# SSM rotation sums on GpSimd, a float32 output operator, q scaled early, reloads into finished heads' slots, and tables in three tiles

## Chip, core and metric

The kernel runs on one core of a Trainium2 chip. The metric is the device time of one execution in microseconds. Five engines work side by side, each through its own instructions in order: TensorE (PE, matmuls; PEld is its weight load), VectorE (DVE), ScalarE (ACT), GpSimd (POOL) and SyncE (SP, which mostly issues DMAs). 'ACTq', 'SPq' and so on are an engine's issuing side.

## What is computed

One layer of a hybrid encoder over 512 positions of width 1024:

```python
h = h + 0.5 * swiglu(rms_norm(h, ffn1_norm), ffn1_w_gate, ffn1_w_up, ffn1_w_down)
u = rms_norm(h, mix_norm)
q, k, v, x_ssm, g_attn, g_ssm = split(u @ w_in)        # 8 q heads, 2 kv heads of 64
q, k = rope(rms_norm(q)), rope(rms_norm(k))
y_attn = softmax(q @ k.T * 64 ** -0.5) @ v @ w_attn_branch
y_s5 = s5(x_ssm, forward) + s5(x_ssm, backward) + ssm_d * x_ssm
z = gelu(y_s5)
z = z * sigmoid(z @ ssm_glu_w + ssm_glu_b)
y_ssm = z @ w_ssm_branch
h = h + (sigmoid(g_attn) * y_attn + sigmoid(g_ssm) * y_ssm) @ w_out
h = h + 0.5 * swiglu(rms_norm(h, ffn2_norm), ...)
h = h + sigmoid(rms_norm(h, ple_norm) @ ple_w_gate) * (p @ ple_w_proj)
```

`s5` is a linear recurrence with complex diagonal states: 32 groups of 16 channels, 64 states each, in both directions.

## The kernel before

Activations are held transposed, features on the 128 partitions and the 512 positions in the free dimension. A float32 matmul is done as three products of halves: `split` (ACT L554, DVE L555) makes a high and a low part, and `mm3` (L569 to L571) multiplies high by high, low by high and high by low. A weight chunk `w` comes in by a DMA on SP (L564) and is split the same way. For the SSM, `split3` (L32 to L38) cuts a float32 tile into three bf16 tiles, two casts on ScalarE and two subtractions on VectorE, and `mm6` (L41 to L45) makes one product of them with six bf16 matmuls.

The span falls into FFN1 (0 to 408 us), the mixing stage (408 to 765), FFN2 (777 to 1122) and the input embedding at the end. FFN1 runs the generator `ssm_params` beside it: after each part of its own work it lets the generator go on by a credit (`side`). The generator makes, from the layer's parameters, four operators of the SSM and writes them to DRAM: `wv` (input), `wo` (output), `m` (within a chunk) and the tables `tb` of rotations and decays. For the tables, eight tiles `tst` of 128x1280 are filled, the last fifth `dv` by VectorE (L303 to L305), the rest by ScalarE (L307 to L309), and written out by ScalarE's queue (L310). The tiles share the tag `w3` with two buffers. On GpSimd's queue go the DMAs that reorder the operators' factors (L240 to L251).

In the mixing stage the SSM runs in 16 blocks of two groups (`ssm_block`). SP loads a block's `wv`, `tbl`, `wo` and `m` (L441 to L449). TensorE forms `pv` with 24 bf16 matmuls. VectorE rotates: `tt` is one 128x512 product (L471), and a difference and a sum of 128x128 make `vv` of it (L472, L473). Two scans over 64 partitions each, forward and backward, make the states W (L481, L482). `te` (L485) and another sum and difference (L486, L487) rotate back and give E. `split3` cuts E in three, and TensorE adds into `py` twelve matmuls of `m` and 24 of `wo`. ScalarE makes GELU of it (Z, L978).

Among the blocks stand other projections: q's norm and rope, the transposes `qt` and `kt`, and the gates, 16 in all. A gate is 24 matmuls of 512 columns (`pi`), a product on VectorE (L835) and a tanh on ScalarE. Behind the blocks the eight heads follow, scores (L957, L958), maximum (L959), its scale (L960), exp (L962, with its scale `rq`), four transposes at a time (`ppt`, L1002) and values (`po`, L1007, L1008); the remaining gates and the SSM branch (`pg`) are run among them as `fill`. Z goes through DRAM to be transposed: SP writes it in eight DMAs (L985), and `z_load` fetches it in four pieces `zT` on GpSimd's queue (L1034) into slots of the normed input `xg`, which the gates read until their end. ScalarE and VectorE split each piece into `z`.

The order of the instructions on each engine is set by a scheduler of the tile framework when the kernel is built; `high_priority` puts the SSM blocks ahead. A tile with `bufs` 1 can be written again only when its last reader is done.

Of the kernel before, what the change touches and what calls it, by code (L numbers as in the profile page):

```python
# [45 lines left out]
def ssm_params(tc, nc, pk_, px, dp, k):  # L46
# [6 lines left out]
    d["wo"] = dp.tile([NB, P, 3 * GB * 2 * P], BF16, name="d_wo")  # L53
# [221 lines left out]
    for gh in range(0, G, GH):  # L275
        T = pw.tile([P, 2, GH, NC_ + 2], F32, tag="T", name=f"T{gh}")
        V.memset(T[:, :, :, 0], 0.0)
        V.memset(T[:, :, :, NC_ + 1], 0.0)
# [4 lines left out]
        n = 1
        tb = pw.tile([P, 2, 2, GH * NC_ // 2], F32, tag="tb", name=f"tbx{gh}")
        while n < NC_:
            br = rkl[:, 0].unsqueeze(2).broadcast_to([P, GH, n])
# [4 lines left out]
            if n < NC_:
                sq = pw.tile([P, 2, GH], F32, tag="sq", bufs=2, name=f"sq{gh}_{n}")
                ta = pw.tile([P, 2, 2, GH], F32, tag="sqt", name=f"sqt{gh}_{n}")
                cmul2(sq[:, 0], sq[:, 1], rkl, rkl[:, 0], rkl[:, 1], ta)
# [42 lines left out]
    for b in range(NB):  # L337
        gs = slice(b * GB, (b + 1) * GB)
        x4 = lambda t: t[:, gs].unsqueeze(3).broadcast_to(sh)
        y4 = lambda t: t[:, gs].unsqueeze(2).broadcast_to(sh)  # L340
# [72 lines left out]
    for b in range(NB):  # L413
# [22 lines left out]
def ssm_prefetch(nc, sp, k, j):  # L436
# [16 lines left out]
def ssm_block(nc, sp, px, pre, U, j):  # L453
# [64 lines left out]
def kernel(  # L518
# [427 lines left out]
    def scores(hd):  # L946
# [273 lines left out]
```

## Time and profile before

| what | value |
|---|---|
| median of three runs | 1187.05 us (1185.81 to 1188.17) |
| the profiled execution's own time | 1185.39 us |
| its span in the profile | 1183.6 us |
| TensorE, matmuls | 1143.2 us busy, 97% of the span |
| TensorE, weight loads (beside matmuls) | 943.5 us, 80% |
| VectorE | 774.0 us, 65% |
| ScalarE | 507.5 us, 43% |
| GpSimd | 58.5 us, 5% |
| mean granted clock of TensorE | 0.987 of full speed |

The busy shares are means over stages that differ much; the windows in the rows below show the stages. A window's row gives each engine's busy time with its number of instructions in brackets, then TensorE's granted clock as a share of full speed, the mean busy share of the DMA engines and what they moved.

### The profile page before, as it was taken

How to read it: one execution, taken by the hardware profiler on the slowest of the kernel's cores; microseconds unless marked ns; L12 is line 12 of the kernel's file. 1: busy time of each engine (PE TensorE's matmuls, PEld its weight loads, DVE VectorE, ACT ScalarE, POOL GpSimd, SP SyncE). 2: the span in 40 equal slices, each digit the busy share in tenths (PEclk: the TensorE clock that was granted, in tenths of full speed). 3: DMA queues.
4: the chain of work that ended last, by engine and by line, in shares of the span. 5: the costliest groups of instructions: out<-in, count | busy, mean ns of one | idle time of the engine just before them, and what ended most of it. 6: DMA issues, size and time to landing. Idle time of an engine off the chain costs nothing.

```text
span 1183.6 us, 16482 instructions
## 1 busy us (share of the span) xinstructions
PE 1143.2 (97%) x6150; PEld 943.5 (80%) x6150; DVE 774.0 (65%) x1574; ACT 507.5 (43%) x919; POOL 58.5 (5%) x95
## 2 busy tenths in 40 slices
PE   8999989999999999978898999999999999999998
PEld 7888868888788888867676788888888888888886
DVE  4986798887589848989666867554443344444542
ACT  6484455444345437443656634342322223223331
POOL 1314100000000000000010000000000000000100
PEclk9999999999999999999997999999999999999999
DMA  8739865545968995887552245333323433323422
GB/s 190 171 92 313 256 221 178 161 142 107 271 228 268 298 193 157 250 251 224 132 86 62 45 105 164 88 98 91 89 74 99 128 100 96 88 64 98 157 57 54
DMA packets 253440, 175.97 MB, mean 149 GB/s; under 512 B 34896, under 2 KB 235792, under 8 KB 253360
## 3 DMA queue, kind: packets, MB, share of 16 engines
q1 hardware_dynamic: 246352, 153.20, 46.1%
q0 software_dynamic: 5392, 15.36, 5.0%
q10 hardware_dynamic: 1616, 6.36, 1.6%
q8 instruction: 48, 0.79, 0.3%
q14 instruction: 32, 0.26, 0.1%
HBM read 148.89 MB, written 37.58 MB: 158 GB/s over the span
## 4 chain that ended last, share of the span: by engine, by line
PE 74%; DVE 9%; DMA 8%; SPq 3%; issue 3%; ACT 2%; POOL 0%; ACTq 0%; DVEq 0%; POOLq 0%
PE pg L569 7%; PE pg L571 7%; PE pg L570 7%; PE pd L569 7%; PE pd L571 7%; PE pd L570 7%; PE pu L571 5%; PE pu L569 5%; PE pu L570 5%; DMA d_tb<-tst 2%; SPq L411 1%; PE pge L571 1%; PE po L569 1%; PE po L570 1%; PE po L571 1%
## 5 line engine op out<-in xcount | busy, mean ns | idle before, releaser
L723 DVE TENSOR_TENSOR t<-pu,rb 128x512 f32<-128x512 f32 x44 | 30.4, 692 | 86.4 <-PE pu L571 86.3
L721 DVE TENSOR_TENSOR t<-pg,rb 128x512 f32<-128x512 f32 x44 | 30.4, 691 | 54.6 <-PE pg L571 52.3
L554 ACT CAST ah<-t 128x512 fp32r<-128x512 f32 x44 | 27.3, 621 | 36.6 <-DVE t L724 35.9
L742 DVE SCALAR_TENSOR_TENSOR h<-pd,h 128x512 f32<-128x512 f32 x32 | 22.1, 690 | 30.5 <-PE pd L571 30.5
L722 ACT ACTIVATE t<-t 128x512 f32<-128x512 f32 x44 | 27.8, 632 | 28.4 <-DVE t L721 27.3
L555 DVE TENSOR_TENSOR al<-t,ah 128x512 fp32r<-128x512 f32 x44 | 30.3, 689 | 6.7 <-ACT ah L554 6.6
L724 DVE TENSOR_TENSOR t<-t,t 128x512 f32<-128x512 f32 x44 | 30.4, 691 | 2.3
L959 DVE TENSOR_REDUCE nb<-sc 128x1 f32<-128x512 f32 x32 | 21.7, 686 | 9.0 <-PE sc L958 8.9
L555 DVE TENSOR_TENSOR pl<-ppt,ph 128x512 fp32r<-128x512 f32 x32 | 22.0, 687 | 7.6 <-ACT ph L554 7.6
L554 ACT CAST ph<-ppt 128x512 fp32r<-128x512 f32 x32 | 18.8, 588 | 18.5 <-PE ppt L1002 18.4
L962 ACT ACTIVATE p<-sc,nb,rq 128x512 f32<-128x512 f32 x32 | 24.9, 781 | 3.8 <-DVE nb L960 3.5
L1125 POOL DMA_DIRECT2D pin<-in_p_dram x8 | 4.1, 524 | 400.4 <-PE pd L570 395.3
L579 ACT ACTIVATE xh<-h,gains 128x512 fp32r<-128x512 f32 x24 | 17.4, 724 | 14.0 <-DVE h L742 13.5
L1007 PE MATMUL po<-ph,vhl 128*128 128x512 f32 x32 | 14.3, 446 | 7.6 <-ACT ph L554 7.6
L43 PE MATMUL py<-E,wol 128*128 128x64 bf16 x384 | 18.6, 199 | 2.6 <-DVE E L36 2.2
L1002 PE MATMUL ppt<-ident,p 128*128 128x128 f32 x128 | 20.8, 277 | 0.0
L1002 PEld LDWEIGHTS ppt<-ident,p 128*128 128x128 f32 x128 | 16.6, 143 | 4.6 <-issue 0.2
L43 PEld LDWEIGHTS <-wol 128*128 128x128 bf16 x384 | 15.0, 101 | 5.3 <-issue 3.8
L43 PE MATMUL pv<-U,wv 128*128 128x64 bf16 x384 | 13.9, 193 | 5.4 <-DMA wv<-d_wv 5.4
L43 PEld LDWEIGHTS <-wv 128*128 128x128 bf16 x384 | 12.1, 98 | 7.8 <-DMA wv<-d_wv 6.0
L580 DVE SCALAR_TENSOR_TENSOR xl<-h,gains,xh 128x512 fp32r<-128x512 f32 x24 | 18.0, 749 | 0.4
L33 ACT CAST E<-vv 128x256 bf16<-128x256 f32 x16 | 6.5, 404 | 25.6 <-DVE vv L487 25.4
(1974 smaller groups left out, 3909.7 us busy)
## 6 DMA issues: line engine op xcount, KB each, us to landing
w<-in_ffn_w_gate_dram SPq DMA_DIRECT2D x44, 512.0 KB
w<-in_ffn_w_up_dram SPq DMA_DIRECT2D x44, 512.0 KB
w<-in_w_in_dram SPq DMA_DIRECT2D x26, 512.0 KB
w<-in_ffn_w_down_dram SPq DMA_DIRECT2D x32, 384.0 KB
w<-in_ffn_w_down_dram SPq DMA_DIRECT2D x32, 320.0 KB
d_wo<-wo SPq DMA_DIRECT2D x8, 768.0 KB
d_wv<-wv SPq DMA_DIRECT2D x8, 768.0 KB
wv<-d_wv SPq DMA_DIRECT2D x16, 384.0 KB
```

The lines of the kernel that those rows point to most:

```text
L43: nc.tensor.matmul(o, a[i], b[j], start=start and n == 0, stop=stop and n == 5)
L554: S.copy(hi, src)
L555: V.tensor_sub(lo, src, hi.bitcast(F32))
L569: T.matmul(o, ah, bh, start=start, stop=False)
L570: T.matmul(o, ah, bl, start=False, stop=False)
L571: return T.matmul(o, al, bh, start=False, stop=stop)
L721: V.tensor_mul(t1, gu[0], rb)
L722: S.activation(t1, t1, AF.Silu)
L723: V.tensor_mul(t2, gu[1], rb)
L724: V.tensor_mul(t1, t1, t2)
L962: S.activation(p_, sc, AF.Exp, bias=nb[:, t:t + 1], scale=rq[:, t, hd:hd + 1], accum_out=sm[:, t:t + 1])
L1002: T.transpose(pt[:, t * P:(t + 1) * P], pr[t][:, kt * P:(kt + 1) * P], ident)
```

## The change

Six edits. The sums of `vv` and E go from VectorE to GpSimd. The `wo` operator is written to DRAM in float32 (512 KB for four groups in place of 768), E is no longer split, and one float32 matmul takes the place of six bf16 ones, four a block. `wv` gets a second buffer in the blocks; in FFN1 the tile `wt` gets a second one, and `bd` and `bd3` go from two to one. The tables are filled in three tiles, `dv`, `st0` and `st1`, each with two buffers and a DMA of its own, `dv`'s on GpSimd's queue. q is multiplied by `rq` right after rope, so that the maximum's product (L960) and the scale of exp go. `zT` is loaded on SP's queue into the slots of q's heads 0 to 3, once each head is done, and `hb` is loaded early.

```diff
-    d["wo"] = dp.tile([NB, P, 3 * GB * 2 * P], BF16, name="d_wo")
+    d["wo"] = dp.tile([NB, P, GB * 2 * P], F32, name="d_wo")
...
         for b in range(gh // GB, (gh + GH) // GB):
-            st = pw.tile([P, TW], F32, tag="w3", bufs=2, name=f"tst{b}")
...
-            dv = v(4)
+            dtb = d["tb"][b].rearrange("p (i n) -> p i n", i=5)
+            dv = pw.tile([P, GB, NC_], F32, tag="dv", bufs=2, name=f"dv{b}")
             V.tensor_copy(dv, e8[:, b * GB:(b + 1) * GB].unsqueeze(2).broadcast_to([P, GB, NC_]))
...
-            for ri in range(2):
-                nc.scalar.copy(v(ri), T[:, ri, g0:g0 + GB, 1:NC_ + 1])
-                nc.scalar.copy(v(2 + ri)[:NS], T[:NS, ri, g0:g0 + GB, 0:NC_])
-                nc.scalar.copy(v(2 + ri)[NS:], T[NS:, ri, g0:g0 + GB, 2:NC_ + 2])
-            nc.scalar.dma_start(d["tb"][b], st)
+            nc.gpsimd.dma_start(dtb[:, 4], dv.rearrange("p g c -> p (g c)"))
+            gs = slice(b * GB - gh, (b + 1) * GB - gh)
+            for i in range(2):
+                st = pw.tile([P, 2, GB, NC_], F32, tag=f"st{i}", bufs=2, name=f"tst{b}_{i}")
+                for ri in range(2):
+                    if i == 0:
+                        nc.scalar.copy(st[:, ri], T[:, ri, gs, 1:NC_ + 1])
+                    else:
+                        nc.scalar.copy(st[:NS, ri], T[:NS, ri, gs, 0:NC_])
+                        nc.scalar.copy(st[NS:, ri], T[NS:, ri, gs, 2:NC_ + 2])
+                nc.scalar.dma_start(dtb[:, 2 * i:2 * i + 2], st.rearrange("p r g c -> p r (g c)"))
...
-    bds = [pw.tile([P, 2, GB, 2, CH], F32, name=f"bd{i}") for i in range(2)]
+    bds = [pw.tile([P, 2, GB, 2, CH], F32, name=f"bd{i}") for i in range(1)]
...
-        wt = pw.tile([P, GB, 2, L, CH], F32, tag="wt", name=f"wo{b}")
+        wt = pw.tile([P, GB, 2, L, CH], F32, tag="wt", bufs=2, name=f"wo{b}")
...
+        nc.sync.dma_start(d["wo"][b], wt.rearrange("p g r l c -> p (g r l c)"))
...
-        nc.sync.dma_start(d["wo"][b], w3.rearrange("p i g r m -> p (i g r m)"))
...
-    wv = sp.tile([P, 3, GM, 2 * P], BF16, tag="wv", name=f"wv{j}")
+    wv = sp.tile([P, 3, GM, 2 * P], BF16, tag="wv", bufs=2, name=f"wv{j}")
...
-    wo = sp.tile([P, 3, GM, 2 * P], BF16, tag="wo", bufs=2, name=f"wol{j}")
+    wo = sp.tile([P, GM, 2 * P], F32, tag="wo", bufs=2, name=f"wol{j}")
...
     V.tensor_mul(tt, b2(pv2), bb(0))
-    V.tensor_sub(vv[:, 0], tt[:, 0, 0], tt[:, 1, 1])
-    V.tensor_add(vv[:, 1], tt[:, 0, 1], tt[:, 1, 0])
+    nc.gpsimd.tensor_sub(vv[:, 0], tt[:, 0, 0], tt[:, 1, 1])
+    nc.gpsimd.tensor_add(vv[:, 1], tt[:, 0, 1], tt[:, 1, 0])
...
-    V.tensor_add(E[:, 0], tt[:, 0, 0], tt[:, 1, 1])
-    V.tensor_sub(E[:, 1], tt[:, 0, 1], tt[:, 1, 0])
-    E3 = [sp.tile([P, 2, N], BF16, tag=f"E{i}", bufs=2, name=f"E3{j}_{i}") for i in range(3)]
-    split3(nc, sp, E, E3, "vv", f"Er{j}", 3)
+    nc.gpsimd.tensor_add(E[:, 0], tt[:, 0, 0], tt[:, 1, 1])
+    nc.gpsimd.tensor_sub(E[:, 1], tt[:, 0, 1], tt[:, 1, 0])
...
-            mm6(nc, o, [wo[:, i, g, ri * P:(ri + 1) * P] for i in range(3)],
-                [e[:, ri, g * NC_:(g + 1) * NC_] for e in E3], False, ri == 1)
+            nc.tensor.matmul(o, wo[:, g, ri * P:(ri + 1) * P], E[:, ri, g * NC_:(g + 1) * NC_],
+                             start=False, stop=ri == 1)
...
+        for t in range(TT):
+            V.tensor_mul(qs[t], qs[t], rq[:, t].unsqueeze(2).broadcast_to([P, NH, HD]))
...
-            V.tensor_mul(nb[:, t:t + 1], nb[:, t:t + 1], rq[:, t, hd:hd + 1])
             p_ = slot(pool_p[hd % 2], "pp", 4, "p")
-            S.activation(p_, sc, AF.Exp, bias=nb[:, t:t + 1], scale=rq[:, t, hd:hd + 1], accum_out=sm[:, t:t + 1])
+            S.activation(p_, sc, AF.Exp, bias=nb[:, t:t + 1], accum_out=sm[:, t:t + 1])
...
+    def z_fetch(m):
+
+        zTs.append(slot(mp, f"q{m}", 1, "zT"))
+        nc.sync.dma_start(zTs[m], zs_d[m * P:(m + 1) * P])
...
-            zT = xs_(4 + m, "l", "zT")
-            nc.gpsimd.dma_start(zT, zs_d[m * P:(m + 1) * P])
...
     for hd in range(NH):
+        for m in {1: (0,), 2: (1, 2), 3: (3,)}.get(hd, ()):
+            z_fetch(m)
         run(values(hd), fill(hd), *([scores(hd + 1)] if hd < NH - 1 else []))
```

The scheduler moves much more than the diff. On VectorE, among the SSM blocks, a pair of blocks before reads:

```order
L485 TENSOR_TENSOR te_6090<-W_6085,tbl_6047 128x512 [waits DVE_49]
L471 TENSOR_TENSOR tt_6175<-pv_6150,tbl_6142 128x512 [waits DMAHW3_49]
L477 MEMSET W_6275 64x1 [waits DVE_49]
L478 MEMSET W_6275 64x1
L486 TENSOR_TENSOR vv_6091<-te_6090 128x128
L487 TENSOR_TENSOR vv_6091<-te_6090 128x128
L34 TENSOR_TENSOR Er_6098<-vv_6091,E_0_6095 128x256 [waits Activation_49]
L472 TENSOR_TENSOR vv_6176<-tt_6175 128x128
L473 TENSOR_TENSOR vv_6176<-tt_6175 128x128
L481 SCALAR_TENSOR_TENSOR W_6180<-tbl_6142,vv_6176 64x256 [waits DMAHW4_49,DVE_49]
L482 SCALAR_TENSOR_TENSOR W_6180<-tbl_6142,vv_6176 64x256
L36 TENSOR_TENSOR E_2_6097<-Er_6098,E_1_6096 128x256 [waits Activation_49]
```

and in the change:

```order
L489 TENSOR_TENSOR te_5807<-W_5802,tbl_5764 128x512 [waits DVE_49]
L475 TENSOR_TENSOR tt_5864<-pv_5839,tbl_5831 128x512 [waits DMAHW1_49,PE_49]
L481 MEMSET W_5936 64x1 [waits DVE_49]
L482 MEMSET W_5936 64x1
L485 SCALAR_TENSOR_TENSOR W_5869<-tbl_5831,vv_5865 64x256 [waits DMAHW2_49,Pool_49]
L486 SCALAR_TENSOR_TENSOR W_5869<-tbl_5831,vv_5865 64x256
```

`tt` is the first rotation's product, `te` the second's, W the scans, and `Er` and `E_2` the split of E. The four sums and two split steps have left VectorE's order; `te` and the next block's `tt` follow one another, and the scan behind them waits for GpSimd (`Pool_49`). On GpSimd, where no work of the blocks stood, now stands for each block:

```order
L476 TENSOR_TENSOR vv_5230<-tt_5229 128x128
L477 TENSOR_TENSOR vv_5230<-tt_5229 128x128
L490 TENSOR_TENSOR vv_5240<-te_5239 128x128
L491 TENSOR_TENSOR vv_5240<-te_5239 128x128
L476 TENSOR_TENSOR vv_5297<-tt_5296 128x128
L477 TENSOR_TENSOR vv_5297<-tt_5296 128x128
```

The `vv` made from `te` is E. The sums stand strictly block by block, all 64 of them, with nothing between them.

On TensorE, where the last gate of the SSM phase ends, before reads (`pi` is a gate, `sc` the first head's scores):

```order
L569 MATMUL pi_5838<-xh_382,w_383h 128x512
L570 MATMUL pi_5838<-xl_383,w_383h 128x512
L571 MATMUL pi_5838<-xh_382,w_383l 128x512
L957 MATMUL sc_6627<-kh_4141,qT_4133 128x512
L958 MATMUL sc_6627<-kl_4143,qT_4133 128x512
L957 MATMUL sc_6634<-kh_4141,qT_4133 128x512
L958 MATMUL sc_6634<-kl_4143,qT_4133 128x512
L957 MATMUL sc_6641<-kh_4141,qT_4133 128x512
L43 LDWEIGHTS wol_6430
L43 MATMUL py_6483<-E_2_6477,wol_6430 128x64
```

and in the change, ahead of the gates that now stand behind the blocks:

```order
L942 MATMUL kt_5070<-ident,kd_5061 128x128 x4
L942 MATMUL kt_5077<-ident,kd_5061 128x128 x4
L571 MATMUL pi_5177<-xh_368,w_377h 128x512
L572 MATMUL pi_5177<-xl_369,w_377h 128x512
L573 MATMUL pi_5177<-xh_368,w_377l 128x512
```

(`kt` are the key transposes), and where these gates end:

```order
L571 MATMUL pi_5678<-xh_382,w_383h 128x512
L572 MATMUL pi_5678<-xl_383,w_383h 128x512
L573 MATMUL pi_5678<-xh_382,w_383l 128x512
L963 MATMUL sc_6243<-kh_4173,qT_4165 128x512
L964 MATMUL sc_6243<-kl_4175,qT_4165 128x512
```

Before, blocks still follow behind the first scores (`py_6483`, the last but one block), and 12 gates stand among the 16 blocks. In the change the last `kt` transpose is behind all blocks; four whole gates (`pi_5177`, `pi_5344`, `pi_5511`, `pi_5678`, 24 matmuls each, of which the first and the last three are shown) come next, and then the first scores. 8 gates stay among the blocks and 4 among the heads.

GpSimd's order before, at the loads of the SSM's output, reads (`r_d` and `R` carry softmax's sums):

```order
L968 DMA r_d_5063<-s_386_6626 128x8x1
L1018 DMA R_6977<-r_d_5063 64x512 x2
L1034 DMA zT_7220<-zs_d 128x512
L968 DMA r_d_5064<-s_428_6890 128x8x1
L1034 DMA zT_7226<-zs_d 128x512
L1034 DMA zT_7232<-zs_d 128x512
```

In the change they stand on SP:

```order
L566 DMA w_7070<-in_w_ssm_branch_dram 128x4x256
L1034 DMA zT_6446<-zs_d 128x512
L566 DMA w_7180<-in_w_ssm_branch_dram 128x4x256
L1034 DMA zT_6563<-zs_d 128x512
L566 DMA w_7260<-in_w_ssm_branch_dram 128x4x256
L566 DMA w_7294<-in_w_ssm_branch_dram 128x4x256
L1034 DMA zT_6565<-zs_d 128x512
L1034 DMA zT_6676<-zs_d 128x512
```

The four `zT` have left the row behind the heads' small transfers; now they stand among the branch weights of SP, each behind a wait for TensorE, the last reader of a head's q.

In FFN1, VectorE's copies into `dv` all stand within the rows 131 to 241 of its order; before, the copies into `tst` stood in the rows 131 to 385.

## Rows read from the trace of the kernel before

**Rows 1.** Page, totals: busy us (share of the span) xinstructions of each engine.
```profile
PE 1143.2 (97%) x6150; PEld 943.5 (80%) x6150; DVE 774.0 (65%) x1574; ACT 507.5 (43%) x919; POOL 58.5 (5%) x95
```

**Rows 2.** Windows: from and to, length, busy us (instructions) of each engine, clock, DMA.
```profile
140.00:160.00 20.00, 14.65 (x56) 10.97 (x55) 16.85 (x37) 12.10 (x27) 0.00 (x0) 0.91 0.60 198
480.00:580.00 100.00, 87.86 (x1088) 74.15 (x1087) 88.46 (x218) 41.69 (x83) 0.76 (x1) 0.97 0.78 231
580.00:640.00 60.00, 49.13 (x241) 38.31 (x240) 37.28 (x73) 35.06 (x68) 6.14 (x10) 0.86 0.46 80
...
960.00:980.00 20.00, 20.00 (x90) 16.55 (x89) 10.08 (x12) 6.56 (x8) 0.00 (x0) 1.00 0.28 83
458.00:582.00 124.00, 111.86 (x1311) 94.03 (x1309) 111.92 (x271) 58.24 (x145) 0.76 (x1) 0.97 0.74 218
```

**Rows 3.** Waits in FFN1, VectorE's and TensorE's: total us, times, longest.
```profile
DVE tst L303 <- DMA d_tb<-tst: 10.4, 3, 6.3
...
PE pd L569 <- ACT ah L554: 5.1, 2, 3.2
```

**Rows 4.** Chain of waits in FFN1: start us, us, what.
```profile
129.79 7.83 DMA d_tb<-tst
...
144.60 0.41 ACT tst L307
```

**Rows 5.** Waits of TensorE at 480 to 580 us.
```profile
PE pv L43 <- DMA wv<-d_wv: 5.4, 4, 2.5
```

**Rows 6.** Chain of waits behind the SSM blocks.
```profile
590.73 11.93 DMA w<-in_w_ssm_branch_dram
...
613.88 12.66 DMA zT<-zs_d
```

**Rows 7.** Waits of ScalarE at 600 to 640 us.
```profile
ACT z L554 <- DMA zT<-zs_d: 9.3, 2, 6.7
```

**Rows 8.** Windows of 5 us, columns as in Rows 2.
```profile
620.00:625.00 5.00, 1.65 (x5) 1.06 (x5) 2.67 (x5) 0.00 (x0) 0.00 (x0) 0.54 0.38 34
625.00:630.00 5.00, 2.12 (x4) 1.30 (x5) 2.79 (x6) 3.44 (x7) 1.05 (x2) 0.50 0.74 232
```

**Rows 9.** Groups by form, VectorE at 458 to 582: busy us, mean ns, idle before.
```profile
L485 DVE TENSOR_TENSOR te<-W,tbl 128x512 f32<-128x512 f32 x16 | 11.0, 688 | 0.2
...
L471 DVE TENSOR_TENSOR tt<-pv,tbl 128x512 f32<-128x512 f32 x16 | 11.0, 686 | 1.9 <-DMA tbl<-d_tb 1.8
L481 DVE TENSOR_TENSOR_SCAN W<-tbl,vv 64x256 f32<-64x256 f32 x16 | 10.9, 680 | 0.2
L34 DVE TENSOR_TENSOR Er<-vv,E 128x256 f32<-128x256 f32 x16 | 6.8, 423 | 4.9 <-ACT E L33 4.8
L36 DVE TENSOR_TENSOR E<-Er,E 128x256 bf16<-128x256 f32 x16 | 6.8, 423 | 1.2 <-ACT E L35 0.9
...
L472 DVE TENSOR_TENSOR vv<-tt 128x128 f32<-128x128 f32 x16 | 4.6, 288 | 0.1
```

**Rows 10.** Groups by form, GpSimd over the whole span.
```profile
L968 POOL DMA_DIRECT2D r_d<-s x4 | 3.7, 922 | 47.7 <-DVE s L967 47.7
...
L670 POOL COPY late<-xt 128x1 f32<-128x1 f32 x1 | 0.2, 183 | 9.9 <-DMA xt<-in_x_dram 9.9
```

**Rows 11.** Chain: pieces of TensorE, with their number of records.
```profile
511.61 0.70 PE pv L43 x24
512.31 0.93 PE py L43 x32
...
1126.15 0.79 PE pm L630 x8
```

**Rows 12.** Windows with much DMA; the last three columns as in Rows 2.
```profile
480.00:500.00 20.00, 18.70 (x239) 15.86 (x238) 19.64 (x61) 7.07 (x14) 0.00 (x0) 1.00 0.87 255
...
485.00:490.00 5.00, 3.69 (x43) 2.93 (x41) 4.88 (x15) 2.18 (x4) 0.00 (x0) 1.00 1.05 308
```

**Rows 13.** ScalarE's exp line: duration in ns min/median/max, first and last start.
```profile
L962 ACT ACT_TABLE_LOAD  x3: 1283/1283/1283, 571.1 to 584.2; - x3
```

More of the change, by code (lines that the diff above doesn't have):

```diff
@@ L297, in ssm_params @@
         for b in range(gh // GB, (gh + GH) // GB):
-            st = pw.tile([P, TW], F32, tag="w3", bufs=2, name=f"tst{b}")
-            g0 = b * GB - gh
             N = GB * NC_
-            v = lambda i, w=1: st[:, i * N:(i + w) * N].rearrange("p (g c) -> p g c", c=NC_)
-            dv = v(4)
+            dtb = d["tb"][b].rearrange("p (i n) -> p i n", i=5)
+            dv = pw.tile([P, GB, NC_], F32, tag="dv", bufs=2, name=f"dv{b}")
             V.tensor_copy(dv, e8[:, b * GB:(b + 1) * GB].unsqueeze(2).broadcast_to([P, GB, NC_]))
@@ L357, in ssm_params @@
             lags(*lag)
-        bd = bds[b % 2]
+        bd = bds[0]
         for dr in range(2):
@@ L361, in ssm_params @@
             nc.scalar.copy(bd[ps, :, :, dr], bb[ps, :, gs])
-        bd3 = pw.tile([P, 3, 2, GB, 2 * CH], BF16, tag="bd3", bufs=2, name=f"bd3{b}")
+        bd3 = pw.tile([P, 3, 2, GB, 2 * CH], BF16, tag="bd3", bufs=1, name=f"bd3{b}")
         split3(nc, pw, bd.rearrange("p r g d c -> p r g (d c)"), [bd3[:, i] for i in range(3)], "r3", f"bdr{b}", 2)
@@ L418, in ssm_params @@
         nc.sync.dma_start(br, b_d[:, :, gs])
-        wt = pw.tile([P, GB, 2, P], F32, tag="wt", name=f"wv{b}")
+        wt = pw.tile([P, GB, 2, P], F32, tag="wt", bufs=2, name=f"wv{b}")
         m1 = pw.tile([P, GB, P], F32, tag="m1", name=f"m1v{b}")
@@ L445, in ssm_prefetch @@
     nc.sync.dma_start(tb[:, 5], src[:, 4, q * NC_:(q + GM) * NC_])
-    wo = sp.tile([P, 3, GM, 2 * P], BF16, tag="wo", bufs=2, name=f"wol{j}")
-    nc.sync.dma_start(wo, d["wo"][b].rearrange("p (i g m) -> p i g m", i=3, g=GB)[:, :, q:q + GM])
+    wo = sp.tile([P, GM, 2 * P], F32, tag="wo", bufs=2, name=f"wol{j}")
+    nc.sync.dma_start(wo, d["wo"][b].rearrange("p (g m) -> p g m", g=GB)[:, q:q + GM])
     mm = sp.tile([P, 3, GM, P], BF16, tag="m", bufs=2, name=f"ml{j}")
@@ L838, in gate @@
         return proj_T(GA0 + m * P, done)
+    hb = mp.tile([P, 4], F32, name="hb")
+    nc.gpsimd.dma_start(hb, w["ssm_glu_b"][0].rearrange("(m p) -> p m", p=P))
     ts = []
@@ L845 @@
     vhl = mp.tile([P, TT, 2, 2, HD], F32R, name="vhl")
-    rq = mp.tile([P, TT, NH], F32, name="rq")
     sx = ExitStack()
@@ L914 @@
         V.tensor_scalar(msq, ssq, 1.0 / HD, EPS, mul, add)
+        rq = qp.tile([P, TT, NH], F32, name="rq")
         rqk = rsqrt_newton(qp, msq, [P, TT, NH + 2], "rqk")
         V.tensor_scalar_mul(rq, rqk[:, :, :NH], HD ** -0.5)
+        for t in range(TT):
+            V.tensor_mul(qs[t], qs[t], rq[:, t].unsqueeze(2).broadcast_to([P, NH, HD]))
         for m in range(NG1):
@@ L1021, in values @@
             split(ohl[hd // 2][0], ohl[hd // 2][1], of)
-    yhl, zs = [], []
+    yhl, zs, zTs = [], [], []
+    def z_fetch(m):
+        zTs.append(slot(mp, f"q{m}", 1, "zT"))
+        nc.sync.dma_start(zTs[m], zs_d[m * P:(m + 1) * P])
     def z_load():
         xs_ = lambda k, c, name, dt=F32: slot(xp, f"x{k}{c}", 1, name, dt)
-        hb = at.tile([P, 4], F32, name="hb")
-        nc.gpsimd.dma_start(hb, w["ssm_glu_b"][0].rearrange("(m p) -> p m", p=P))
         V.tensor_scalar_mul(hb, hb, 0.5)
@@ L1032, in z_load @@
         for m in range(4):
-            zT = xs_(4 + m, "l", "zT")
-            nc.gpsimd.dma_start(zT, zs_d[m * P:(m + 1) * P])
             zh, zl = xs_(m, "h", "z", F32R), xs_(m, "l", "z", F32R)
-            split(zh, zl, zT)
-            zs.append((zT, zh, zl))
+            split(zh, zl, zTs[m])
+            zs.append((zTs[m], zh, zl))
     def half(ww, mc, x, done):
```

## The prediction, made before the changed kernel ran

> **What bounds the kernel now.** I read the totals first, then the span cut into windows, then waits and chain where a window falls short. TensorE is busy for 1143.2 of 1183.6 us [rows 1], and in FFN2 a 20 us window holds 90 matmuls of 512 columns, 0.222 us each, without a gap [rows 2]. So only time in which TensorE stands still, or runs at a lower granted clock, can be won without removing matmuls. I call a window's length less its busy time times its granted clock 'lost'. By [rows 2] that is 20 − 14.65 × 0.91 = 6.7 us at 140 to 160, 100 − 87.86 × 0.97 = 14.8 at 480 to 580, and 60 − 49.13 × 0.86 = 17.7 at 580 to 640: about 39 us in three places, and the change touches all three.
>
> The first place: the tables of the SSM, built beside FFN1. VectorE stands for 10.4 us in three waits for the DMA that writes a table tile back, the longest 6.3, and the down-projection waits 5.1 us in two waits for ScalarE's cast `ah` [rows 3]. The chain ties them together: a 7.83 us piece of that DMA from 129.79 on, then VectorE's work that had queued, then at 144.60 ScalarE's copies into the next table tiles [rows 4]; in ScalarE's order `ah` stands behind those.
>
> The second: the 16 SSM blocks. At 458 to 582 VectorE is busy for 111.92 of 124 us and TensorE for 111.86 [rows 2]. Both are near full, and VectorE's work of a block is one chain: product, two sums, two scans, product, two sums, split. The weights of the blocks come late too: TensorE waits 5.4 us in four waits for `wv` [rows 5].
>
> The third: GELU, the SSM output's way through DRAM, and softmax's start. The chain goes from the writes of Z over a weight transfer of 11.93 us to GpSimd's `zT` load, whose 12.66 us run from 613.88 [rows 6]. ScalarE, in order, waits 9.3 us for it in two waits [rows 7], with the casts of probabilities for TensorE behind it. At 620 to 625 TensorE is busy for 1.65 of 5 us; at 625 to 630 it is busy for 2.12, at a granted clock of 0.50 [rows 8], the lower of its two levels, 1.2 GHz.
>
> **The change part by part.**
>
> *Tables in three tiles.* VectorE's copy `dv` gets a tile of its own whose DMA goes out on GpSimd's queue, and by the order it stands far ahead of its old place, so VectorE no longer stands behind the big write. Moved past is GpSimd's queue: the eight small DMAs stand there ahead of the A and B operators' loads, in time in which GpSimd only issues. ScalarE can wait in VectorE's place: its copies need the tile of two groups earlier written out. But the next burst of copies starts at 144.60, 15 us after the DMA's 129.79, and that took 7.83 [rows 4], so I take no wait. Gain 6 of the 6.7 lost; bounds 0 and 6.7.
>
> *The sums on GpSimd.* Removed from VectorE: 64 sums of 0.288 us, 18.4 us, and with the split of E 32 steps of 0.423, 13.5 us [rows 9]. VectorE's 111.92 becomes 80.0 over the same work; scaling q adds four 128x512 products at 0.686 [rows 9], 2.7 us. Against that stands a new round trip. By the order VectorE goes `te`, `tt` of the next block, two memsets, and then stands at the first scan until GpSimd has done E's two sums and the next `vv`'s two. A block's chain is two scans of 0.680, `te` 0.688 and about four GpSimd sums of t each (some of it under `tt`): 2.1 + 4t. Behind the waiting scan are queued the gates' products and weight splits, and for those TensorE waits. No row of before has a sum on GpSimd. The nearest are a 128x1 copy at 0.183 as the lower end, and its longest DMA issue in this stage, 0.922, as the upper [rows 10]; VectorE's 0.288 for the same sum lies between. I take t = 0.4, near VectorE's: 3.7 us a block, some 4.1 with the hand-overs, 66 us for sixteen, less than the other bounds below. The Trainium skill (GPSIMD Engine Reference, 3.1 Elementwise — side-by-side cycle accounting) gives 4497 ns for a GpSimd sum of 2048 float32 elements; an estimate scaled from it to 128 elements is 0.28 us without the dispatch, and the block would be 3.2 us by it. No run here shows it yet.
>
> *One float32 product for six bf16 ones.* 24 bf16 products a block become four in float32. The bf16 ones go 32 in 0.93 us, 0.029 each: 384 take 11.1 us. The nearest float32 row is the norms' column sum, whose eight records are four products, each with weights to load: 0.79 us, 0.2 each [rows 11]. So 64 × 0.2 = 12.8, and TensorE loses 1.7 us; it gains nothing. Bounds 0 (the new ones as dear as the old) and 3.3 (0.225 each).
>
> *The phase of the blocks.* The order moves four gates (96 matmuls, 21.4 us) from among the last blocks to behind the last, ahead of the first head's scores. With the blocks stay 8 gates, 192 × 0.222 = 42.7; `pv` 16 × 0.70 = 11.2 [rows 11]; the `m` products 192 × 0.029 = 5.6; the float32 ones 12.8; transposes about 1: 73 us for TensorE. VectorE needs at most 82.7, less what goes with the four gates. DMA moves 1.22 MB a block (wv 384, tables 384, wo 256, m 192 KB) and 8 to 10 gate weights of 512 KB, 24 MB: 79 us at the 308 GB/s of a full 5 us, 95 at the 255 of a whole 20 us window [rows 12]. I take 83, where VectorE and the fast DMA figure meet. Lost: 83 − 73 = 10, against 14.8: a gain of 5, with 15 (nothing lost) and −7 (95 us) as bounds. What lets the DMA keep up is the second `wv` buffer: the 5.4 us of waits are for a tile that could not be loaded before its last reader had ended.
>
> *Four gates behind the blocks, and `zT` in q's slots.* The gates' 21 us of TensorE work now cover the last GELU, Z's writes and the first exponentials. `zT` goes out on SP behind the first of `w_ssm_branch`, into slots that finished heads leave, while before it waited on GpSimd for slots that the gates still read. The small products of nb and rq go too, and gelu and exp no longer take turns: three of the table loads are exp's, 1.283 us each [rows 13], and the order keeps one. Behind a late `zT` ScalarE's casts would still stand, and the price is then the old wait. I take 3.7 us lost in place of 17.7: a gain of 14; bounds 7 (softmax's start stays as it is) and 17.
>
> *Sum.* 1185.39 (the profiled run; its span is 1183.6, and it is 1.66 us below the median of the three) − 6 − 5 − 14 + 1.7 = 1162.1. I forecast **1162**.
>
> **The rivals.**
>
> *GpSimd's round trip becomes the bound, and the kernel slower.* Place: the first scan of each block. Sixteen times 2.1 + 4t passes 83 us when t is over 0.77. Without the blocks the change is worth −18.3, and a phase of 88 is worth nothing; so it comes out slower from a phase of 106 us, t = 1.13. At t = 1.5 the phase is 130 and the total 1185.4 − 18.3 + 42 = 1209. Against it: the GpSimd rows end at 0.922, which gives 93 us and 1172. For it: no sum was seen there. Chance 5%.
>
> *VectorE and GpSimd hold each other up.* If no sum may run beside any VectorE instruction, the phase is 82.7 less the four gates' share (some 7) plus 64 × 0.4, 101 us, and the total 1180; halfway 1171. Nothing of before shows either, since GpSimd does no sum there. For it speaks how full VectorE is; against it, that by the order most sums run while VectorE stands at the scan. The Trainium skill (SBUF — State Buffer, Who interferes with whom) has a rule of this kind, against this change: the two engines share a port pair which one instruction holds to its end. Chance 12%.
>
> *DMA is the bound.* 95 us at 255 GB/s: lost 22, total 1174. For it: the busy share of 1.05 in [rows 12]. Chance 12%.
>
> *FFN1 does not gain*, since ScalarE now waits for the table tiles with `ah` behind it: 1168. Chance 10%. *The third place does not do what it should* (`zT` still late, softmax as before): 1169. Chance 8%. *All of the second place is won*, a phase near 73: 1152. Chance 6%.
>
> **How the numbers follow.** The forecast, with 1154 to 1170 around it, has the other 47%. The range 1148 to 1178 takes in all rivals but a slow round trip and the worse half of the mutual hold-up, about 1 in 10, and on the low side all bounds at their good ends at once (1185.4 − 6.7 − 15 − 17 = 1147), somewhat less. A measurement of this kernel tells 0.2%, 2.4 us, from no change. Slower has the round trip's 5% and 1% of the hold-up; within 0.2% lies where a slow round trip meets the gains, 3%; faster has 91%.
>
> **What would show it.** In the profile after: no VectorE wait on a table DMA in FFN1 and TensorE over 19 us busy at 140 to 160; GpSimd sums of 0.3 to 0.5 us and a block every 5 us; VectorE waiting on GpSimd at the first scan, about 1 us a block; a granted clock of 1.00 through the heads; `zT` landed before ScalarE asks for it. Wrong would make it: sums over 1 us, scans or products on VectorE longer than 0.69, `wv` and table waits of the old size, or float32 products over 0.23 us.

## The result and the profile after

The changed kernel takes 1173.21 us (median of four, 1172.21 to 1177.81), before 1186.43 us beside it: a ratio of 0.9895, interval 0.9866 to 0.9923, or about 12 us faster. The forecast was 1162, the range 1148 to 1178. The profiled execution is the longest of the four, 1177.81 us with a span of 1176.0, 7.6 us less than the profiled one of before. A second profile of it (below) took 1175.54.

The totals, with the columns of [rows 1]:

```profile
span 1176.0 us, 15927 instructions
...
PE 1147.8 (98%) x5894; PEld 948.3 (81%) x5894; DVE 750.9 (64%) x1449; ACT 487.5 (41%) x883; POOL 94.7 (8%) x163
```

The three places, with the columns of [rows 2]:

```profile
140.00:160.00 20.00, 18.40 (x82) 14.91 (x81) 15.49 (x27) 12.68 (x27) 0.00 (x0) 1.00 0.79 254
455.00:580.00 125.00, 113.62 (x1027) 95.75 (x1025) 91.19 (x172) 40.09 (x108) 34.02 (x64) 0.93 0.72 208
580.00:640.00 60.00, 58.54 (x287) 47.04 (x288) 43.40 (x68) 41.18 (x89) 4.88 (x7) 1.00 0.29 80
```

Lost, as the prediction reckons it: 1.6 us in the first place (6.7 before), 1.5 in the third (17.7 before). The second, 455 to 580, lost 125 − 112.86 × 0.97 = 15.5 before:

```profile
455.00:580.00 125.00, 112.86 (x1296) 94.79 (x1295) 111.93 (x271) 59.13 (x161) 0.76 (x1) 0.97 0.75 222
```

Now it is 125 − 113.62 × 0.93 = 19.3. VectorE has 21 us less work there, and TensorE gets nothing from it. Its standing time is nearly the same, 11.4 us against 12.1; what has grown is the time at the lower clock (a mean of 0.93 against 0.97).

The waits show where TensorE stands. First the third place (ScalarE at 600 to 640), where the 9.3 us of [rows 7] are 0.2:

```profile
ACT z L556 <- DMA zT<-zs_d: 0.2, 1, 0.2
```

Then TensorE at 455 to 580, against [rows 5], and VectorE there:

```profile
PE py L43 <- DMA ml<-d_m: 3.9, 3, 2.2
PE py L497 <- POOL vv L490: 2.5, 1, 2.5
PE kt L942 <- DVE kl L557: 2.0, 1, 2.0
PE pv L43 <- DMA wv<-d_wv: 1.5, 3, 0.9
...
DVE W L485 <- POOL vv L477: 9.9, 10, 2.1
```

The wait for `wv` has fallen from 5.4 to 1.5, but waits for `ml`, GpSimd's E and the key transposes came in its place. Windows of 5 us (columns as in [rows 8]) show what follows:

```profile
510.00:515.00 5.00, 3.44 (x37) 2.54 (x35) 3.30 (x7) 1.35 (x2) 1.91 (x6) 1.00 1.10 328
515.00:520.00 5.00, 3.79 (x54) 3.50 (x55) 4.13 (x8) 0.00 (x0) 2.09 (x4) 0.69 0.71 205
520.00:525.00 5.00, 5.00 (x22) 4.32 (x20) 2.83 (x7) 0.55 (x2) 1.85 (x5) 0.50 0.92 279
525.00:530.00 5.00, 5.00 (x50) 3.98 (x49) 3.05 (x7) 1.68 (x2) 1.55 (x4) 0.79 0.76 238
```

TensorE stands for 2.8 us between 510 and 520, and is then busy without a gap for 10 us at a granted clock of 0.50 and 0.79 (5 × 0.50 + 5 × 0.21): 3.6 us more, lost while it looks fully busy.

The sums on GpSimd, by form at 455 to 580 (busy us, mean ns, idle before), and two stretches of its timeline (start, us, what):

```profile
L476 POOL TENSOR_TENSOR vv<-tt 128x128 f32<-128x128 f32 x16 | 10.2, 638 | 61.3 <-DVE tt L475 58.9 <-PE py L497 1.5 <-DVE W L482 0.8
L477 POOL TENSOR_TENSOR vv<-tt 128x128 f32<-128x128 f32 x16 | 9.9, 617 | 0.0
L491 POOL TENSOR_TENSOR vv<-te 128x128 f32<-128x128 f32 x16 | 8.1, 507 | 0.0
L490 POOL TENSOR_TENSOR vv<-te 128x128 f32<-128x128 f32 x16 | 7.4, 461 | 49.3 <-DVE te L489 44.5 <-DVE rqk L593 2.6 <-PE pi L572 2.3
```

```profile
463.12 0.46 POOL L490 TENSOR_TENSOR vv<-te 128x128 f32<-128x128 f32 x1 [2.89 <-DVE te L489]
463.54 1.02 POOL L491 TENSOR_TENSOR vv<-te 128x128 f32<-128x128 f32 x1
...
531.38 0.46 POOL L490 TENSOR_TENSOR vv<-te 128x128 f32<-128x128 f32 x1 [4.83 <-DVE te L489]
531.80 0.45 POOL L491 TENSOR_TENSOR vv<-te 128x128 f32<-128x128 f32 x1
```

```profile
462.96 0.68 DVE L475 TENSOR_TENSOR tt<-pv,tbl 128x512 f32<-128x512 f32 x1
463.56 0.68 DVE L882 TENSOR_TENSOR qs<-rp,rq 128x512 f32<-128x512 f32 x1
...
531.16 0.68 DVE L475 TENSOR_TENSOR tt<-pv,tbl 128x512 f32<-128x512 f32 x1
```

A sum takes 0.46 us. Beside VectorE's `tt`, which reads `pv` from PSUM, it still does (463.12, 531.38). Beside the sum of two SBUF tiles at 463.56 it takes 1.02. All four lines together are busy for 35.6 us, 6 more than 64 × 0.46.

### The profile page after: what moved, and what is told of

Read it like the earlier page. It is cut to its first block, busy times and chain, and to the rows that moved or that the text cites. A ratio compares the mean times of both kernels' runs of the same rounds, so it can differ in the third digit from the quotient of the medians.

```text
span 1176.0 us, 15927 instructions
## 1 busy us (share of the span) xinstructions
PE 1147.8 (98%) x5894; PEld 948.3 (81%) x5894; DVE 750.9 (64%) x1449; ACT 487.5 (41%) x883; POOL 94.7 (8%) x163
## 4 chain that ended last, share of the span: by engine, by line
PE 68%; DVE 10%; issue 7%; DMA 7%; ACT 3%; SPq 3%; POOL 1%; ACTq 0%; POOLq 0%; DVEq 0%
PE pg L571 6%; PE pg L572 6%; PE pg L573 6%; PE pd L571 6%; PE pd L573 6%; PE pd L572 6%; PE pu L571 5%; PE pu L573 5%; PE pu L572 5%; DMA w<-in_ffn_w_up_dram 3%; PE pi L571 2%; PE pi L572 1%; PE pi L573 1%; SPq L415 1%; PE po L572 1%
## 5 line engine op out<-in xcount | busy, mean ns | idle before, releaser
L965 DVE TENSOR_REDUCE nb<-sc 128x1 f32<-128x512 f32 x32 | 21.3, 682 | 11.4 <-PE sc L964 11.4
L497 PE MATMUL py<-vv,wol 128*128 128x64 f32 x128 | 21.0, 294 | 3.1 <-POOL vv L490 2.5
L581 ACT ACTIVATE xh<-h,gains 128x512 fp32r<-128x512 f32 x24 | 17.3, 723 | 14.7 <-DVE h L744 14.3
L967 ACT ACTIVATE p<-sc,nb 128x512 f32<-128x512 f32 x32 | 21.9, 692 | 1.7 <-DVE nb L965 1.0
L497 PEld LDWEIGHTS py<-vv,wol 128*128 128x128 f32 x128 | 18.0, 204 | 4.0 <-POOL vv L490 2.8
L485 DVE TENSOR_TENSOR_SCAN W<-tbl,vv 64x256 f32<-64x256 f32 x16 | 10.9, 680 | 9.9 <-POOL vv L477 9.9
L837 DVE TENSOR_TENSOR ts<-pi,rb 128x512 f32<-128x512 f32 x8 | 5.5, 688 | 18.1 <-PE pi L573 18.1
```

The costliest lines, as they stand in the source:

```text
L497: nc.tensor.matmul(o, wo[:, g, ri * P:(ri + 1) * P], E[:, ri, g * NC_:(g + 1) * NC_], start=False, stop=ri == 1)
```

## The experiments

Each kernel ran beside the kernel before, whose medians were 1185.87 to 1186.60; medians of 4 to 12 runs. 'Lost' is from one profile each: in FFN1 at 130 to 180 us, where the first place lies, in the blocks at 455 to 580 and behind them at 580 to 700. 'Gates' are those among the SSM blocks by the order (13 means 12 whole and the start of one, 10 means 9 and the start of one).

| kernel | median us | ratio (interval) | lost in FFN1 | blocks | behind | gates |
|---|---|---|---|---|---|---|
| before | 1186.43 | 1 | 6.7 | 15.5 | 19.0 | 13 |
| the change | 1173.21 | 0.9895 (0.9866 to 0.9923) | 1.6 | 19.3 | 2.5 | 8 |
| e0 the change again | 1175.18 | 0.9911 (0.9890 to 0.9932) | 1.7 | 21.2 | 1.4 | 8 |
| e1 sums on VectorE | 1175.79 | 0.9918 (0.9898 to 0.9937) | 6.0 | 17.8 | 1.8 | 10 |
| e2 vv on VectorE | 1175.97 | 0.9918 (0.9896 to 0.9940) | 8.8 | 14.9 | 3.1 | 8 |
| e3 one wv buffer | 1175.06 | 0.9904 (0.9885 to 0.9924) | 5.0 | 12.6 | 5.4 | 13 |
| e4 e3 with bf16 operator | 1176.83 | 0.9917 (0.9891 to 0.9942) | 7.5 | 17.0 | 5.5 | 13 |
| f1 tables only | 1179.77 | 0.9949 (0.9931 to 0.9967) | 3.4 | 16.3 | 16.3 | 13 |
| f2 zT only | 1179.88 | 0.9936 (0.9911 to 0.9960) | 9.2 | 17.7 | 7.8 | 13 |
| f3 zT and q | 1174.91 | 0.9905 (0.9877 to 0.9932) | 5.0 | 13.0 | 6.4 | 13 |
| g1 tables, zT, q | 1173.91 | 0.9891 (0.9864 to 0.9917) | 0.0 | 18.9 | 4.5 | 13 |
| g2 g1 and float32 operator | 1169.67 | 0.9842 (0.9816 to 0.9867) | 4.9 | 9.5 | 3.6 | 13 |
| g3 g1 and GpSimd sums | 1174.97 | 0.9903 (0.9880 to 0.9925) | 4.2 | 20.7 | 7.6 | 13 |
| g4 change, three ml | 1177.91 | 0.9933 (0.9911 to 0.9956) | 3.8 | 21.4 | 3.1 | 8 |

**Is the loss in the blocks a matter of one run?** The change once more, with nothing edited.

> The changed kernel itself once more, as the yardstick for the runs beside it. In the trace of it that I have (1177.8 us, the slowest of its four runs) the TensorE time lost between 470 and 560 us is 18 us, as much as before, and of that 7.7 us is a lower granted clock; the waits there are for ml (3.9 us), GpSimd's E (2.5), key transposes (2.0) and wv (1.5). Theory A (the clock made that run slow, the mechanism is the same in all): this trace shows the same waits and less low clock, near 1173 us. Rival B (the waits differ from run to run): another set of waits, the clock following them.

1175.18 us. The same three waits lead (TensorE at 455 to 580):

```profile
PE py L43 <- DMA ml<-d_m: 4.5, 5, 1.4
PE py L497 <- POOL vv L490: 2.2, 1, 2.2
PE kt L942 <- DVE kl L557: 2.0, 1, 2.0
```

The low clock after a stand is there again: 0.51 at 515 to 520, 0.80 at 520 to 525. So half of theory A holds: the waits belong to the kernel, not to one run. The other half fell: the clock in the blocks was no better than in the longest run (0.92 against 0.93).

**Who pays in the blocks?** Three edits of the change.

```diff
 e1, both pairs of sums; e2, the pair of vv alone
-    nc.gpsimd.tensor_sub(vv[:, 0], tt[:, 0, 0], tt[:, 1, 1])
+    V.tensor_sub(vv[:, 0], tt[:, 0, 0], tt[:, 1, 1])
...
 e3
-    wv = sp.tile([P, 3, GM, 2 * P], BF16, tag="wv", bufs=2, name=f"wv{j}")
+    wv = sp.tile([P, 3, GM, 2 * P], BF16, tag="wv", name=f"wv{j}")
```

> The changed kernel with all 64 sums back on VectorE, everything else as changed. The prediction's theory (VectorE's work bounds the blocks, the sums' 18.4 us on it are what is saved): slower than the changed kernel by 2 to 9 us, with VectorE again busy for 90% of the blocks' phase. Rival 1 (the round trip to GpSimd costs what the sums save: VectorE waits 9.9 us at the first scan in the trace of the change, and sums beside VectorE instructions with two SBUF inputs last up to 1.44 us in place of 0.46): within 2 us, or up to 4 faster. Rival 2 (DMA bounds the phase, so no engine's work counts): within 2 us, with the same waits for ml, wv and tables.

> The changed kernel with the two vv sums of a block back on VectorE and only E's two on GpSimd. The block's chain on VectorE loses the wait for GpSimd (about two sums of 0.46 plus hand-over, against two of 0.29), and VectorE gets 9.2 us of work. If the round trip is the bound: faster than the changed kernel by 2 to 6 us. If VectorE's work is the bound: slower by 1 to 5. If DMA is the bound: within 1.5 us.

> The changed kernel with one wv buffer in the blocks in place of two. By the order this alone puts 13 gates back among the blocks, as before the change, with the first head's work right behind the last block. If the gain of the third place (14 us at 580 to 640) comes from the four gates that cover GELU, Z's writes and the first exponentials: slower than the changed kernel by 6 to 14 us, TensorE standing still behind the blocks. If it comes from zT's early load and q's early scale: slower by 0 to 5 us, only by the waits for wv (5.4 us before).

All three stand within 1 us of e0, 1175.06 to 1175.97. For e1 the 2 to 9 us slower that follow from the prediction's theory did not come: with VectorE busy for 103.30 us in the blocks' window, the kernel was as fast as with 91. e2 did not shorten the chain to any gain. e3 did not lose the 6 to 14 us that the four gates behind the blocks were to be worth: 'behind' rose to 5.4, but the blocks' loss fell to 12.6. With one buffer the scheduler puts 13 gates back among the blocks; that these are what lowers the loss there is a reading, since the buffer and the gates changed together.

**The float32 operator.** e3 with the operator in three bf16 parts and E split:

```diff
-            nc.tensor.matmul(o, wo[:, g, ri * P:(ri + 1) * P], E[:, ri, g * NC_:(g + 1) * NC_],
-                             start=False, stop=ri == 1)
+            mm6(nc, o, [wo[:, i, g, ri * P:(ri + 1) * P] for i in range(3)],
+                [e[:, ri, g * NC_:(g + 1) * NC_] for e in E3], False, ri == 1)
```

> The changed kernel with one wv buffer and the output operator in three bf16 parts, E split again: against the changed kernel with one wv buffer (1175.06 us) it undoes the float32 operator alone. The float32 products cost TensorE 64 x 0.23 us in place of 384 x 0.029, 3.6 us more, but save VectorE 13.5 us and ScalarE 12.9 in the blocks' phase. If VectorE's work bounds the phase: slower by 3 to 10 us. If the phase is bound by loads and the clock: faster by 0 to 4 us.

1176.83, 1.8 us slower than e3: less than these intervals tell apart, and between the two expectations. g1 and g2 below ask the same with the sums on VectorE.

**The parts on the kernel before.** f1 has the three tiles of the tables alone, f2 `z_fetch` and `hb` alone, f3 f2 and q's early scale.

> The kernel before with the tables in three tiles as its only change. By the prediction: faster than before by 3 to 7 us, with no VectorE wait on a table write and TensorE over 18 us busy at 140 to 160. Rival (ScalarE or the weights' DMAs stand where VectorE stood; in the runs with the sums on VectorE TensorE waited 4.6 and 5.7 us for ah in FFN1 though the tables were in three tiles): within 2 us of before.

> The kernel before with zT reloaded on SP into finished heads' slots (and the bias loaded early) as its only change. Third place by the prediction: the wait for zT is most of it, TensorE's 16 us lost at 580 to 700 fall by 8 to 12, and the kernel is faster by that. Rival (the order of exp, gelu and the first heads, which q's early scale and the gates behind the blocks changed, is what counts): faster by 0 to 4, the loss at 615 to 635 staying or moving.

> The kernel before with zT reloaded early and q scaled early, the rest as before. If the early scale is worth its table loads and small products: 2 to 5 us faster than with zT alone. If it only adds 2.7 us to a full VectorE in the blocks' phase and takes them back at softmax: the same as with zT alone within 2 us.

f1 gains 6 us, as predicted. f2 gains 7.6 by its ratio (6.3 by the medians), just under its 8 to 12. Its profile shows 7.8 lost behind the blocks in place of 19.0, with the blocks no better (17.7). Before, TensorE waited at 580 to 700 for ScalarE's cast `ph`, and ScalarE's casts stood behind its wait for `zT`; in f2 little of it is left:

```profile
PE po L1007 <- ACT ph L554: 7.6, 3, 5.7
```

```profile
PE po L1009 <- ACT ph L554: 0.7, 2, 0.4
```

f3 adds 5 by the medians, the upper end for the early scale, though the two intervals overlap. Of that the profiles show 1.4 behind the blocks; the rest of their difference lies in the blocks (4.7) and in FFN1 (4.2), which the two kernels share. So `zT` and q alone give as much as the whole change, and how it divides between them is less sure.

**What the rest adds to tables, zT and q.** g1 is these three parts; g2 adds the float32 operator with its FFN1 buffers; g3 adds the 64 sums on GpSimd; g4 is the change with this edit:

```diff
-    mm = sp.tile([P, 3, GM, P], BF16, tag="m", bufs=2, name=f"ml{j}")
+    mm = sp.tile([P, 3, GM, P], BF16, tag="m", bufs=3, name=f"ml{j}")
```

> The kernel before with three parts of the change together: tables in three tiles, zT reloaded early, q scaled early. The SSM blocks stay as before. If the parts add (tables alone -6, zT and q -11 against before): 1167 to 1170 us, faster than the whole change, whose other parts (sums on GpSimd, float32 operator, second wv buffer) then cost 4 to 7 us. If the table gain and the others overlap or drown in what differs from run to run: 1173 to 1176, and the other parts are worth nothing either way.

> The same with the float32 operator added (E not split, wt and bd buffers as in the change), the sums on VectorE, one wv buffer. TensorE gets 3.6 us more work, VectorE 13.5 and ScalarE 12.9 less. If the operator's products are what the change pays: 3 to 5 us slower than tables, zT and q alone. If the freed VectorE pays them back: within 1.5 us, or faster.

> Tables, zT and q with only the 64 sums moved to GpSimd besides, operator and wv buffer as before. If the round trip and the sharing between the two engines cost what the move saves: within 1.5 us of tables, zT and q alone. If they cost more: 2 to 6 us slower, with VectorE waiting at the scans and TensorE waiting for E. If VectorE's work bounds the blocks: 3 to 8 faster.

> The changed kernel with three ml buffers in place of two. TensorE waits 3.9 to 4.5 us for ml in the blocks of the change, and 8 to 9 us more go there in a lower granted clock after it has stood. If those waits (loads that come too late for want of a buffer) make the second place: faster than the changed kernel by 3 to 8 us, the ml waits gone and the clock at 1.00 for most of 510 to 560. If the loads only come late in another tile (wv, tables, operator): within 1.5 us, the same loss with other names.

g1 came to 1173.91: 11 and 6 made 13, by the second of the two expectations. That the gains overlap is not shown, since the intervals of f1, f3 and g1 together leave room for a plain sum. g2 is the fastest kernel here, 1169.67, its runs 1162.55 to 1170.30; all runs of the change lie above (1172.21 to 1177.81). With its FFN1 buffers the operator is worth 4 us here (by the ratios 6, the two intervals just overlapping), so what it saves more than pays for the float32 products. Its windows, blocks and behind:

```profile
455.00:580.00 125.00, 117.86 (x1076) 98.67 (x1074) 108.63 (x244) 52.37 (x131) 0.00 (x0) 0.98 0.69 204
580.00:700.00 120.00, 118.82 (x560) 96.24 (x561) 87.11 (x131) 66.90 (x133) 11.15 (x18) 0.98 0.39 95
```

and all TensorE waits of 0.8 us or more in its blocks:

```profile
PE pv L43 <- DMA wv<-d_wv: 2.5, 2, 1.9
PE po L1012 <- ACT ph L556: 0.9, 1, 0.9
PE py L497 <- DVE vv L477: 0.8, 1, 0.8
PE sc L963 <- DVE ts L837: 0.8, 1, 0.8
```

g2 differs from e3 only in the sums, and from e1 only in the `wv` buffer. So GpSimd's sums cost 5.4 us there (1169.67 to 1175.06) and the second buffer 6.1 (to 1175.79); by the ratios, each beside its own runs of before, it is 7 and 9. The two together, which is the change, cost no more than each alone. In e1 the waits at 455 to 580 are for the loads that come beside the second `wv`:

```profile
PE py L43 <- DMA ml<-d_m: 3.0, 5, 1.5
PE py L497 <- DMA wol<-d_wo: 2.9, 4, 1.4
```

In g2 these are 0.2 each, against its 2.5 for `wv`. On the bf16 operator (g3 against g1) the sums cost 1 us, which can't be told from nothing; the 3 to 8 us faster that go with a bound by VectorE's work did not come. g3's blocks wait 8.7 us for `wv`:

```profile
PE pv L43 <- DMA wv<-d_wv: 8.7, 4, 3.7
PE py L43 <- DMA ml<-d_m: 2.3, 1, 2.3
PE py L43 <- DVE E L36: 1.1, 2, 0.6
```

In g4 the `ml` waits are gone from the list, and the loss is not; the median is 2.7 us over e0, which the intervals don't tell apart:

```profile
PE pv L43 <- DMA wv<-d_wv: 5.2, 2, 3.1
PE py L497 <- POOL vv L490: 3.5, 1, 3.5
PE kt L942 <- DVE qT L933: 2.7, 1, 2.7
```

## Why the prediction was right, and where not

*The third place: right, for a part of its reasons.* Forecast a gain of 14; the windows at 580 to 640 give 17.7 − 1.5 = 16. That `zT` no longer waits is most of it (f2: 19.0 to 7.8 behind the blocks); the early scale takes it to 6.4 in f3. The table loads are as the order had them, one for exp:

```profile
L967 ACT ACT_TABLE_LOAD  x1: 1283/1283/1283, 579.0 to 579.0; - x1
```

The four gates behind the blocks cover softmax's start, as the prediction said, but e3 and g2, without them, lose 5.4 and 3.6 behind the blocks, against 1.4 and 2.5 in e0 and the change and 1.8 in e1, which differ from them in the buffer alone. The gates are worth some 2 to 4 us there, but e3 without them is no slower than e0.

*The phase of the blocks: the step that failed.* Forecast a gain of 5; the change lost 3.8 more than before in its own profile and 5.7 more in e0's. The phase took 92 us, from the first `tt` at 457.7 to the last `py` at 549.4, not 83. The DMA reached the lower of my two figures, not the higher:

```profile
480.00:500.00 20.00, 18.35 (x197) 15.62 (x196) 19.46 (x47) 3.26 (x7) 7.17 (x12) 1.00 0.86 264
500.00:520.00 20.00, 17.22 (x199) 14.77 (x198) 15.05 (x30) 3.92 (x6) 7.84 (x17) 0.92 0.86 253
520.00:540.00 20.00, 20.00 (x195) 17.26 (x193) 13.30 (x27) 4.43 (x8) 6.91 (x16) 0.82 0.87 262
```

So the rival 'DMA is the bound' (1174) came nearest the time, and e1 and e2, where the engines' work changed and the time did not, speak for it. But it isn't the bytes alone: g2 moves the same loads as e3 and as e1 and is 5 to 6 us faster, and in g4 a spared wait for one load came back as a wait for another. What I had wrong is to take the longest of three bounds and let the others run beside it. My reading is that load, round trip and VectorE miss each other in single blocks, and their waits add: the blocks lose 9.5 in g2, 12.6 with the sums on GpSimd (e3), 17.8 with the second buffer (e1), and 19.3 and 21.2 with both, from one profile each. And I counted the four gates as moved without price. They were long matmuls that gave TensorE work between the blocks. With 8 or 10 gates there the granted clock of the blocks' window was 0.92, 0.92, 0.93, 0.93 and 0.95 (g4, e0, change, e1, e2), with 13 it was 0.93 to 0.99 (g3 0.93, the others 0.96 or more). The count of gates goes with the `wv` buffer by the scheduler's choice; no run moved the gates alone, so that the gates hold the clock up is the reading of five profiles against nine, not a test.

*The sums on GpSimd.* The duration was well placed: 0.46 against 0.4, with 0.64 and 0.62 for `vv`'s mean. The wait is of the size too: 9.9 us for GpSimd in ten waits, 0.6 a block, where I had about 1. Missed was that the VectorE time which the sums had taken bought nothing (e1): the chain lost 1.15 us of sums a block on VectorE and got four of 0.46 on GpSimd. The rival 'VectorE and GpSimd hold each other up' is real and small in the trace, some 6 us of GpSimd's time; what it costs the kernel was not separated from the round trip. The Trainium skill (SBUF — State Buffer, Who interferes with whom) has the two engines exclude each other over a shared port pair. The trace agrees where VectorE reads two SBUF tiles (1.02 us beside 463.56) and shows none beside `tt`, which reads PSUM. The Trainium skill (GPSIMD Engine Reference, 3.1 Elementwise — side-by-side cycle accounting) led to an estimate of 0.28 us without the dispatch. The measured 0.46 decides.

*The float32 product: mis-sized.* Four products (eight records) take 0.92 us in the chain of the change, 0.23 each, just over my upper bound of 0.225; 64 of them 14.7, 3.6 us more than the bf16 ones, not 1.7:

```profile
532.15 0.92 PE py L497 x8
```

By busy time the difference is less, 2.3: 20.0 us for all of them in g2 (450 to 580), 17.7 for the bf16 ones in g1. The row that I took the 0.2 from, `pm`, has one column a product; these have 64, and whether that makes the difference wasn't tried. Yet in g2 the operator gains 4 us where the sums stay on VectorE. E is ready there without the four split steps, and the `wo` load is a third smaller; which of the two does it was not separated.

*FFN1: right in size, not in constancy.* The change's profile gained 5.1 at 140 to 160, and f1, the tables alone, 6 us of time. TensorE's 18.40 us busy there is under the 19 that I named as a sign. And ScalarE now waits there for weights, at 110 to 160:

```profile
ACT w_121h L556 <- DMA w<-in_ffn_w_up_dram: 5.9, 1, 5.9
ACT w_137h L556 <- DMA w<-in_ffn_w_down_dram: 3.7, 1, 3.7
```

Before, its waits there for `w_136h` and `w_137h` were 1.9 and 0.5. The FFN1 of the change, e0, e3, e1 and e2 is instruction for instruction the same; `w_137h` waited 3.7, 1.3, 6.2, 7.0 and 7.6 us in them, and the down-projection behind it 1.6, 1.7, 3.6, 4.6 and 5.7 for `ah`, as against the 5.1 of [rows 3] (g4 does not quite fit this row, with 0.7 and 2.4). TensorE lost 1.6, 1.7, 5.0, 6.0 and 8.8 us at 130 to 180 in the same order, so in e1 and e2 little or nothing is left of the gain. The DMA engines have no room there:

```profile
100.00:140.00 40.00, 40.00 (x178) 33.14 (x177) 29.85 (x122) 18.51 (x37) 15.36 (x24) 1.00 0.99 312
```

So DMA is still in the way there, late with a weight now where it held VectorE's tile, and how much differs from run to run. The three profiles of the old FFN1 (before, f2, f3) lost 6.7, 9.2 and 5.0; the three with the tables alone (f1, g1, g3) 3.4, 0.0 and 4.2; the eight that also have one `bd` buffer and two `wt` (the change, e0 to e4, g2, g4) 1.6 to 8.8. Whether those buffers give part of the gain back wasn't tried and stays open.

*The sum.* From 1185.39: −5.0 (FFN1: 6.7 to 1.7), +5.7 (blocks), −17.6 (behind: 19.0 to 1.4), +3.6 (float32) and +0.5 (the first 30 us) give 1172.6, beside e0's profiled 1175.54; 3 us stay unplaced. Of the 11 us between forecast and result, the blocks are 11 by themselves (9 in the change's own profile); the errors in the others nearly cancel. That the change came out faster rests on the third place. The result lies outside 1154 to 1170, which I had put around the forecast, and inside the range because that took in the rivals: the range held, the phase's mechanism did not.

## What to carry to other kernels

An engine that is 90% busy is not yet the bound: before its work is moved, look for the waits of the engine that sets the end, and for what its freed time would release. A second buffer can cost more than the wait it removes, when it lets a scheduler pull long matmuls out from between short dependent ones and brings other loads late: here it cost 6 us (e1 against g2). When several parts are changed together, run the parts: here two of them gave as much as the whole, and leaving two out made a better kernel (1169.67 us).

## What was not expected of the hardware

A GpSimd sum of two 128x128 float32 tiles took 0.46 us alone and up to 1.44 beside VectorE instructions on two SBUF tiles. In the four cases here, the one that started second ran longer. At 458.28 VectorE's 128x1024 split began first: it took its usual 1.21, and the sum 1.36. At 481.80 a sum began just before the split: that sum took 0.46, the split 1.53, and the next sum, now behind the split, 1.44. The other two splits of the blocks that met sums went the same ways, at 515.73 (1.22) and 470.27 (1.53). GpSimd, then VectorE:

```profile
458.45 1.36 POOL L476 TENSOR_TENSOR vv<-tt 128x128 f32<-128x128 f32 x1 [56.95 <-DVE tt L475]
...
481.80 0.46 POOL L476 TENSOR_TENSOR vv<-tt 128x128 f32<-128x128 f32 x1 [0.42 <-DVE W L482]
482.22 1.44 POOL L477 TENSOR_TENSOR vv<-tt 128x128 f32<-128x128 f32 x1
```

```profile
458.28 1.21 DVE L557 TENSOR_TENSOR w_353l<-w,w_353h 128x1024 fp32r<-128x1024 f32 x1
...
481.81 1.53 DVE L557 TENSOR_TENSOR w_357l<-w,w_357h 128x1024 fp32r<-128x1024 f32 x1
```

And the same FFN1 program lost between 1.6 and 8.8 us at 130 to 180 in five profiles (the change, e0, e3, e1, e2).
